# Seven block products for the gate and up projections of three SwiGLUs

## The chip, the cores and the metric

The kernel runs on one NeuronCore of a Trainium2 chip. The metric is the device time of one execution in microseconds (us), less being better. The engines are named as in the profile: PE (TensorE, with its weight loads as PEld), DVE (VectorE), ACT (ScalarE), POOL (GpSimd) and SP (SyncE, which here only issues DMAs).

## The reference

One inference step of two layers over 640 tokens of 1024 features, in float32. Each layer is a SwiGLU, a mixer (layer 0: convolution beside a gated MLP; layer 1: windowed attention) and a second SwiGLU, each with its own norms, shift, scale and gate:

```python
def swiglu(h, wg, wu, wd):
    return (jax.nn.silu(h @ wg) * (h @ wu)) @ wd

def pre(x, m, g, slot):
    h = rms_norm(x, g)
    return h * (1 + m[:, 3 * slot + 1][:, None, :]) + m[:, 3 * slot][:, None, :]

def residual(x, y, m, g, slot, weight):
    return x + weight * m[:, 3 * slot + 2][:, None, :] * rms_norm(y, g)
```

`wg` and `wu` are 1024 x 2816, `wd` is 2816 x 1024. `m` is the modulation, `silu(cond) @ w_mod + b_mod`, for each layer and two condition vectors. There are four SwiGLUs; the code calls them `ffn(l, i)`, in the order (0,0), (0,1), (1,0), (1,1), with the mixers after (0,0) and (1,0).

## The kernel before, in words

Every matmul operand is split into two parts, `hi` and `lo`, so that three matmuls on TensorE (`mm3`: hi*hi, hi*lo, lo*hi) make one product of float32 quality. `h`, the input of a sub-layer, lies with features on partitions: eight chunks `k` of 128 features, each [128, 640 tokens] in two parts. The hidden 2816 features are 22 chunks `j`, in four parts of 5, 5, 6 and 6 (`PARTS`).

For each `j` of an `ffn`, a *unit* is run on the token group GA (tokens 0 to 383) and one on GB (384 to 639). `proj2` does gate and up together: 8 chunks x 2 x 3 = 48 matmuls of 384 columns for GA, 48 of 256 for GB. `glu` empties them: ACT silu of the gate, DVE times the up, ACT copy to `hi`, DVE subtract to `lo`. The weights of `j` come by `wload`: one DMA of 512 KB from SP into a `raw` tile (three of these), ACT makes `hi` (a tile `w`, six slots), DVE makes `lo`. After each unit `background(1)` runs one `mod_chunk`: a 512 KB load of modulation weights into a `raw` tile and two custom DVE reductions of 1024 elements, work for a later sub-layer taken from a queue.

After the chunks of a part the down projection follows: for both halves of the features and the five token tiles, 3 matmuls of 512 columns for each chunk, added to `y` in SBUF by DVE (by ACT copy in the first part). After the last part comes `tail` (or `last_tail` at the very end): `drain` runs what is left in the queue of modulation chunks, then `last(t)` makes the last part's products of token tile t, both halves, adds them to `y`, and the norm of y, the gate row (`ggrow`, a row spread to all partitions by DMA), the residual (`resid`), the norm of x (`scale`) and the transposes into the next `h` (`turn`) follow, woven with the products of the tiles behind.

What sets the order: instructions of PE, DVE and ACT are issued in the order in which they are written (a wrapper, `InOrder`, ties each to the one before). DMAs go to SP's or POOL's queue, where a scheduler places them. Tiles of a kind share a few slots; whoever takes a slot waits for the last reader of the tile that had it.

Of the kernel before, what the change touches and what calls it, by code (L numbers as in the profile page):

```python
# [11 lines left out]
ALU = mybir.AluOpType  # L12
# [65 lines left out]
class Core:  # L78
    """the NeuronCore; tensor, vector and scalar engine in written order"""
# [7 lines left out]
class Builder:  # L87
    def __init__(self, tc, a, ctx):
# [22 lines left out]
    # Slots of a tag are handed out in the order in which their tiles are first written here. Upper and  # L111
    # lower parts come from different engines, so that they have tags of their own.
# [25 lines left out]
    def split(self, src, hi, lo):  # L138
# [45 lines left out]
    def fetch(self, key, dram, nblk, blk=P):  # L184
        """wload ahead of its use; take() returns it"""
# [3 lines left out]
    def fetch_ahead(self, key, dram, nblk, blk=P):  # L189
        """fetch() with the split left to the two closures that are returned: upper part, lower part"""  # L190
# [22 lines left out]
    def proj2(self, ws, h, g, inserts=None):  # L213
        """two projections together, feature chunk by feature chunk; inserts: {k: emitted before chunk k}"""
# [9 lines left out]
    def proj_tok(self, ps, h, w, t):  # L224
        """ps [128 tokens of tile t, n] = h^T w"""
# [5 lines left out]
    def rsqrt_ops(self, ssq, scale, engine=None):  # L231
        """1/sqrt(ssq * scale + eps) on a few columns: the result and the instructions. engine: of the iterations"""
# [3 lines left out]
        # v holds -1/2 of the argument, the first guess comes from its bits  # L236
# [48 lines left out]
    def turn(self, tiles, c):  # L285
        """PSUM [128 features of chunk c, tokens] from the normalised x"""
# [5 lines left out]
    def tail(self, last, nxt, fetches):  # L292
        """last(t): (closures for the last products of the sub-layer for token tile t, [closures that add the two
        halves to y]). Norms, residual and the next sub-layer's input h follow. What is left of h is in four
        dictionaries: closures to be called before the feature chunks of the next sub-layer's first three units on
        GA and of its first on GB. fetches: closures that start the loads of the next sub-layer's first weights
        and return the two closures that split them."""
# [6 lines left out]
        def sq(t, what, s=None):  # L304
            # sum of squares of x or y
# [13 lines left out]
        def both(tx, ty):  # L319
            # the columns of x[tx] and y[ty] together  # L320
# [64 lines left out]
        # the last tile: what follows its products goes between those of the next sub-layer's first three units  # L385
# [9 lines left out]
        def step(tiles=None, c=None):  # L395
            # transposes of a chunk; upper and lower parts of the one before
# [72 lines left out]
    def last_tail(self, last):  # L469
        """as tail(), for the last sub-layer"""  # L470
# [34 lines left out]
    def mod_final(self, l, slot, what):  # L505
        """what: 0 shift and scale, 1 gate"""
# [16 lines left out]
    def gate_rows(self, l, slot):  # L523
        """gg as rows along the features, the same on every partition"""
# [3 lines left out]
        row = self.sm(P, "grow")[:16]  # L528
# [3 lines left out]
        nc.sync.dma_start(out=self.ggrow.rearrange("p a b -> p (a b)"), in_=rows.to_broadcast([P, 2 * D]))  # L532
# [16 lines left out]
    def glu(self, pg, pu, out, g):  # L549
        """out (hi, lo) columns g = silu(pg) * pu"""  # L550
# [6 lines left out]
    def ffn(self, l, i, h, lead, nxt, fetches, started=None):  # L557
        nc, a = self.nc, self.a
# [101 lines left out]
    def conv_gmlp(self, h, lead, nxt, fetches):  # L660
# [46 lines left out]
        def shifted(c):  # L707
            # 32 channels x 4 shifts on the partitions, for the convolution on the tensor engine
# [70 lines left out]
        def mix(c, copy=lambda out, x: nc.scalar.activation(out=out, in_=x, func=AF.Copy)):  # L779
            # position mixing; what follows the products is returned as closures  # L780
# [72 lines left out]
        # LayerNorm over the conv channels, then swish  # L853
# [38 lines left out]
        for n, f in enumerate(parts):  # L892
# [3 lines left out]
            if n == 3:  # L896
                # from here on the products overwrite the normalised channels
# [40 lines left out]
        # the sines have the sign that they need with the partner  # L938
# [7 lines left out]
    def attention(self, h, lead, nxt, fetches):  # L946
# [4 lines left out]
        # keys of chunk 8 + n: latent tiles 1 and 2, cached ones, latent tiles 3 and 4, so that those of any window  # L951
        # lie side by side; the prompt's
# [29 lines left out]
        def rope(s, pos, on_act=False):  # L982
            """closures; the sum of each is left until the products of the next"""
# [660 lines left out]
```

## Time and profile before

| | |
|---|---|
| time, three runs | 2369.91, 2371.31 and 2374.71 us; median 2371.31 |
| span of the profiled execution | 2369.2 us |
| PE busy | 2343.9 us, 99% of the span, 14484 matmuls |
| DVE busy | 1354.3 us, 57% |
| ACT busy | 833.5 us, 35% |
| POOL busy | 111.4 us, 5% |
| HBM | 248.97 MB read, 106 GB/s over the span |
| granted TensorE clock | 0.996 |

The profiled execution has a span of 2369.2 us beside runs of 2369.91 to 2374.71 us, so it stands 2 us below their median. Busy time counts an engine's own instructions; a busy PE is a PE with matmuls in its pipe. In the views, a line names the engine, the operation, output tile, input tiles and their shapes; in a timeline the first two columns are start and duration, in a window table a cell is the busy time with the number of instructions in parentheses. Nearly all instructions carry the line of the `InOrder` helper (L68), so they are told apart by tile names and shapes.

### The profile page before, as it was taken

To read this page: it belongs to the slowest core of one execution; us is meant where nothing else is said; L and a number is where in the kernel's file an instruction comes from. 1 tells how busy PE (TensorE), PEld (TensorE's weight loads), DVE (VectorE), ACT (ScalarE), POOL (GpSimd) and SP (SyncE) were. 2 spreads that over 40 slices of the span, in tenths; PEclk is the share of its full clock that TensorE was granted. 3 is DMA by queue.
4 is the path that set the end of the run, shared out by engine and by line. 5 is a ranking of instruction groups with operands and counts; after the bars stand their busy time and mean duration, and the time that the engine had idled before them with its cause. 6 is when DMAs were issued, how large, how long until landed. Compare 5 with 4: busy or idle time off the path is not lost.

```text
span 2369.2 us, 35411 instructions
## 1 busy us (share of the span) xinstructions
PE 2343.9 (99%) x14484; PEld 2147.5 (91%) x14484; DVE 1354.3 (57%) x2419; ACT 833.5 (35%) x1507; POOL 111.4 (5%) x191
## 2 busy tenths in 40 slices
PE   9999999999999999999999999999899999999998
PEld 7999999999789899989899999998866798989897
DVE  5556665668775566523755666656888652333235
ACT  5322222363354221213532212225468553212122
POOL 1000000021100000000100000002220010000000
PEclk9999999999999999999999999999999999999999
DMA  7343444413223444422224444352000222222221
GB/s 290 117 141 134 152 136 163 137 56 101 73 86 98 134 159 131 147 87 90 67 89 139 151 142 160 134 171 75 28 21 17 92 76 85 72 81 81 80 73 70
DMA packets 85026, 256.82 MB, mean 108 GB/s; under 512 B 9824, under 2 KB 11744, under 8 KB 84096
## 3 DMA queue, kind: packets, MB, share of 16 engines
q1 hardware_dynamic: 83984, 252.74, 32.0%
q8 instruction: 113, 1.85, 0.3%
q0 software_dynamic: 880, 1.83, 0.2%
q14 instruction: 49, 0.40, 0.1%
HBM read 248.97 MB, written 2.93 MB: 106 GB/s over the span
## 4 chain that ended last, share of the span: by engine, by line
PE 94%; DVE 3%; POOL 1%; ACT 1%; issue 1%; DMA 1%; SPq 0%; DVEq 0%; POOLq 0%; ACTq 0%
PE ps L68 94%; DVE tmp L68 1%; DVE w L68 1%; DVE Y L68 1%; POOL nwq L68 1%; DVE act L68 0%; DMA X<-x 0%; DVE X L68 0%; DMA act<-wmod 0%; POOL nwy L68 0%; ACT w L68 0%; ACT Y L68 0%; DVE nwy L68 0%; DVE nwq L68 0%; ACT act L68 0%
## 5 line engine op out<-in xcount | busy, mean ns | idle before, releaser
L68 PE MATMUL ps<-act,w 128*128 128x384 f32 (+4 forms) x9984 | 1479.5, 314 | 8.2 <-DVE w L68 6.8
L68 PEld LDWEIGHTS ps<-act,w 128*128 128x128 f32 (+2 forms) x9984 | 1425.0, 186 | 32.8 <-issue 15.8
L68 PE MATMUL ps<-w,act 128*128 128x512 f32 (+1 forms) x3480 | 782.9, 384 | 3.1 <-ACT tmp L68 3.1
L68 PEld LDWEIGHTS ps<-w,act 128*128 128x128 f32 x3480 | 627.4, 189 | 136.3 <-ACT tmp L68 3.5
L68 DVE TENSOR_TENSOR w<-raw,w 128x1024 fp32r<-128x1024 f32 (+1 forms) x313 | 365.1, 1199 | 151.4 <-ACT w L68 149.9
L68 ACT ACTIVATE w<-raw 128x1024 fp32r<-128x1024 f32 (+1 forms) x313 | 315.5, 1030 | 367.5 <-PE ps L68 146.9
L68 DVE CUSTOM_DVE_ANT_0 scr<-raw,cbc 128x1024 bf16<-128x1024 f32 x256 | 312.9, 1222 | 12.0 <-DMA raw<-wmodT 6.9
L68 DVE TENSOR_TENSOR tmp<-tmp,ps 128x384 f32<-128x384 f32 (+1 forms) x176 | 85.7, 487 | 401.2 <-ACT tmp L68 357.1
L68 ACT ACTIVATE tmp<-ps 128x384 f32<-128x384 f32 (+2 forms) x198 | 83.7, 425 | 652.4 <-PE ps L68 652.0
L68 DVE TENSOR_TENSOR act<-tmp,act 128x256 fp32r<-128x256 f32 (+2 forms) x306 | 135.3, 448 | 133.7 <-ACT act L68 132.5
L68 DVE TENSOR_TENSOR Y<-Y,ps 128x512 f32<-128x512 f32 x140 | 95.6, 686 | 192.9 <-PE ps L68 192.7
L68 ACT ACTIVATE act<-tmp 128x256 fp32r<-128x256 f32 (+3 forms) x304 | 128.3, 433 | 124.1 <-DVE tmp L68 123.9
L68 ACT ACTIVATE Y<-ps 128x512 f32<-128x512 f32 (+2 forms) x96 | 50.8, 532 | 147.6 <-PE ps L68 147.1
L68 ACT ACTIVATE tmp<-ps,sh,G 128x256 f32<-128x256 f32 (+1 forms) x120 | 60.3, 525 | 22.7 <-PE ps L68 22.7
L68 ACT ACTIVATE tmp<-Y 128x1024 bf16<-128x1024 f32 (+2 forms) x39 | 35.1, 901 | 71.4 <-DVE Y L68 71.4
L68 DVE SCALAR_TENSOR_TENSOR act<-act,cw,act 128x640 f32<-128x640 f32 (+14 forms) x60 | 54.5, 909 | 1.8
L68 ACT ACTIVATE Y<-X 128x1024 f32<-128x1024 f32 x30 | 31.8, 1059 | 54.3 <-DVE X L68 50.7
L68 PE MATMUL ps<-ident,Y 128*128 128x128 f32 x260 | 46.7, 273 | 2.6 <-DVE Y L68 2.2
L68 DVE CUSTOM_DVE_ANT_0 raw<-ps,ggrow 128x384 f32<-128x384 f32 (+1 forms) x64 | 41.1, 680 | 12.8 <-PE ps L68 11.4
L68 POOL TENSOR_TENSOR nwq<-nwy 128x1 f32<-128x1 f32 (+1 forms) x30 | 17.9, 595 | 613.2 <-DVE nwy L68 611.7
L68 PEld LDWEIGHTS ps<-ident,Y 128*128 128x128 f32 x260 | 34.4, 140 | 11.7 <-DVE Y L68 3.9
L68 ACT ACTIVATE raw<-raw,nmx 128x384 f32<-128x384 f32 (+1 forms) x64 | 42.2, 669 | 1.0 <-DVE nmx L68 0.9
(149 smaller groups left out, 758.6 us busy)
## 6 DMA issues: line engine op xcount, KB each, us to landing
raw<-wmodT SPq DMA_DIRECT2D x128, 512.0 KB, 3.8
raw<-wg SPq DMA_DIRECT2D x88, 512.0 KB, 4.5
raw<-wu SPq DMA_DIRECT2D x88, 512.0 KB, 3.6
raw<-wd SPq DMA_DIRECT2D x80, 512.0 KB, 4.0
act<-wmod SPq DMA_DIRECT2D x24, 256.0 KB, 6.5
ggrow<-grow SPq DMA_DIRECT2D x6, 1024.0 KB, 4.6
raw<-win SPq DMA_DIRECT2D x12, 512.0 KB, 3.7
raw<-wqkv SPq DMA_DIRECT2D x10, 512.0 KB, 3.8
```

Source lines behind the costliest of these rows:

```text
L68: i = method(*args, **kw)
```

## The change

For the last three SwiGLUs, (0,1), (1,0) and (1,1), `ffn` hands over to a new function, `ffn_seven`. The first four chunks (`LEAD`) still run as units. For the chunks j = 4 to 21 the gate and up products of one j, seen as a 2x2 block product (features 0-511 and 512-1023; tokens 0-319 and 320-639), are made by seven block products p1 to p7 in place of eight. Each is 4 feature chunks x 3 matmuls of 320 columns, 84 matmuls for one j.

- **Sums of h.** `block_sums` makes, for each of four pairs of chunks, two new sums of the blocks of `h`, split in two parts: two adds of 640 columns (hi + lo), four operations of 320, two splits of 640. They stand between the feature chunks of the units (1,GB), (2,GB) and (3,GA), one for each feature chunk.
- **Room.** The sums and two more raw tiles (`rawx`) take the SBUF region of `x`, `y` and `ggrow`. `x` is written to DRAM before (5 DMAs of 512 KB), the down projections of the parts go to DRAM (`ys`: ACT copy to a `tmp` tile, then a DMA, adding from the second part on, on POOL's queue), and `hold_xy` brings all back when the last p4 is done: ten loads of y of 256 KB, five of x of 512 KB, then `ggrow` (1 MB).
- **Weights.** A new tensor `ws` in DRAM holds the blocks of gate and up. For each j: `load_gate` (512 KB, raw `g`), `load_sums` (512 KB on SP into `rawx`, then on POOL's queue 512 KB that are added to it in the DMA: raw `s`), and `load_up` (512 KB for two j, raw `u`). DVE makes the sums `t` from s and g (two adds of 512). `g`, `s` and `t` are split for each j, `u` for every second: 3.5 splits for a j in place of 2.
- **Order.** A round of j runs p1(j), p3(j-1), p6(j), p4(j-1), p5(j), p2(j), p7(j); p1, p6, p5 and p3 of a j add up in one PSUM tile, which is copied after p1, p6 and p5 (evacuations e1, e6, e5) and goes through silu after p3 (e3). e2 adds and takes silu, e7 and e4 subtract, then the product and its split. `prep(j+1)` puts the weight work of the next j between these, with `background(1)` once a round.
- Comments and docstrings are gone as well.

```diff
+SEVEN = [(0, 1), (1, 0), (1, 1)]
+LEAD = 4
+HT = T // 2
...
+    def hold_xy(self, saved=None):
+        self.turn_region("xy")
...
+            for t in range(NT):
+                for half in range(2):
+                    hf = slice(half * 512, half * 512 + 512)
+                    self.nc.sync.dma_start(out=self.y[t][:, hf], in_=ys[t, half])
+                self.nc.sync.dma_start(out=self.x[t], in_=xs[t])
...
     def ffn(self, l, i, h, lead, nxt, fetches, started=None):
+        if (l, i) in SEVEN:
+            return self.ffn_seven(l, i, h, lead, nxt, fetches)
...
+        def whole(n, c):
+            t[n] = self.tmp(T)
+            hi, lo = (u.bitcast(F32) for u in h[c])
+            V.tensor_tensor(out=t[n], in0=hi, in1=lo, op=ALU.add)
...
+        return [lambda: whole(0, pair), lambda: whole(1, pair + 4), first, second, lambda: split(2), lambda: split(3)]
...
+        def load_sums(j):
+
+            w = a["ws"][l, i, j]
+            r = self.rawx()
+            nc.sync.dma_start(out=r, in_=w[:, 512:1536])
+            nc.gpsimd.dma_start(out=r.rearrange("p (a b) -> p a b", a=2),
+                                in_=w[:, 1536:2048].unsqueeze(1).to_broadcast([P, 2, 512]), accum_op=ALU.add)
+            raws["s", j] = r
...
+            def s2():
+                t = raws["t", j] = self.raw(D)
+                V.tensor_tensor(out=t[:, 0:512], in0=raws["s", j][:, 512:1024], in1=raws["g", j][:, 512:1024], op=ALU.add)
+
+            def s4():
+                t = raws["t", j]
+                V.tensor_tensor(out=t[:, 512:1024], in0=t[:, 0:512], in1=raws["g", j][:, 0:512], op=ALU.add)
...
+            return [[lambda: load_up(j) if two else None, s2, s4], [g[0]], [g[1], t[0]], [t[1]] + (nxt_g if first else []),
+                    [s[0], lambda: self.background(1)], [s[1], lambda: load_sums(j + 2) if j + 2 < NJ else None],
+                    u + ([] if first else nxt_g)]
...
+        def product(n, j, ps, start, stop):
+            w = wts.pop((n, j))
+            for p in range(4):
+
+                self.mm3(ps, tuple(u[:, p * P:(p + 1) * P] for u in w), moving[n](p), start and p == 0, stop and p == 3,
+                         skip_group_check=True)
...
+        unit(1, GB, sums_between())
+        weights(3)
+        unit(2, GB, sums_between())
+        for g in GROUPS:
+            unit(3, g, sums_between())
+        run(tops)
...
+                if j > j0:
+                    steps = [(p1, j), (p3, j - 1), (p6, j), (p4, j - 1), (p5, j), (p2, j), (p7, j)]
+                else:
+                    steps = [(p1, j), (p2, j), (p6, j), (p7, j), (p5, j), None, None]
...
+                        o = self.tmp(512)
+                        copy(o, ps)
+                        if pi == 0:
+                            nc.sync.dma_start(out=ys[t, half], in_=o)
+                        else:
+                            nc.gpsimd.dma_start(out=ys[t, half], in_=o, accum_op=ALU.add)
...
+                            else:
+                                self.background(2 if t < 3 else 1)
...
+                self.hold_xy((xs, ys))
+                self.spread_rows(rows)
```

The next listings show three places of the engines' orders. Numbers behind names tell tiles of one kind apart.

**ACT, inside ffn(1,1).** Before, one chunk of the part 5 to 9: the `hi` of two weight tiles, then silu and `hi` of the unit on GA, then of the one on GB.

```order
L68 ACTIVATE w_19060<-raw_19058 128x1024
L68 ACTIVATE w_19066<-raw_19064 128x1024
L68 ACTIVATE tmp_19122<-ps_19072 128x384
L68 ACTIVATE act_19070<-tmp_19122 128x384
L68 ACTIVATE tmp_19177<-ps_19127 128x256
L68 ACTIVATE act_19070<-tmp_19177 128x256
```

After, the round of j = 12, the first after a pair of `u` was split. In order: hi of u, e1(12), hi of g for 13, silu e3(11), hi of t for 13 (w_20592), e6(12), hi of the product of 11, hi of s for 13, e5(12), silu e2(12).

```order
L72 ACTIVATE w_20537<-raw_20429 128x1024
L72 ACTIVATE tmp_20572<-ps_20543 128x320
L72 ACTIVATE w_20575<-raw_20541 128x1024
L72 ACTIVATE tmp_20446<-ps_20414 128x320
L72 ACTIVATE w_20592<-raw_20557 128x1024
L72 ACTIVATE tmp_20573<-ps_20543 128x320
L72 ACTIVATE act_20623<-tmp_20446 128x640
L72 ACTIVATE w_20627<-rawx_20409 128x1024
L72 ACTIVATE tmp_20573<-ps_20543 128x320
L72 ACTIVATE tmp_20572<-tmp_20572 128x320
```

Between e1 and e6 of one PSUM tile (ps_20543) stand now two splits of weights and a silu; the slot of w_20592 was that of the u pair before, which p4(11) is the last to read.

**DVE, ffn(0,1) at the start of the third or fourth chunk.** Before: the last steps of the units (1,GB) and (2,GB), `lo` of two weight tiles, then the unit (3,GA).

```order
L68 TENSOR_TENSOR tmp_7272<-tmp_7272,ps_7223 128x256
L68 TENSOR_TENSOR act_6961<-tmp_7272,act_6960 128x256
L68 TENSOR_TENSOR tmp_7327<-tmp_7327,ps_7278 128x256
L68 TENSOR_TENSOR act_7043<-tmp_7327,act_7042 128x256
L68 TENSOR_TENSOR w_7335<-raw_7332,w_7334 128x1024
L68 TENSOR_TENSOR w_7341<-raw_7338,w_7340 128x1024
L68 TENSOR_TENSOR tmp_7396<-tmp_7396,ps_7347 128x384
L68 TENSOR_TENSOR act_7345<-tmp_7396,act_7344 128x384
```

After, the end of the fourth pair of sums, the units (3,GA) and (3,GB), the two adds that make t for j = 4, and `lo` of g (w_7553) and of t (w_7557) for j = 4.

```order
L72 TENSOR_TENSOR tmp_7432<-tmp_7432,tmp_7440 128x320
L72 TENSOR_TENSOR tmp_7432<-tmp_7424,tmp_7432 128x320
L72 TENSOR_TENSOR sum_7458<-tmp_7440,sum_7457 128x640
L72 TENSOR_TENSOR sum_7468<-tmp_7432,sum_7467 128x640
L72 TENSOR_TENSOR tmp_7477<-tmp_7477,ps_7403 128x384
L72 TENSOR_TENSOR act_7401<-tmp_7477,act_7400 128x384
L72 TENSOR_TENSOR tmp_7532<-tmp_7532,ps_7483 128x256
L72 TENSOR_TENSOR act_7401<-tmp_7532,act_7400 128x256
L72 TENSOR_TENSOR raw_7549<-rawx_7229,raw_7227 128x512
L72 TENSOR_TENSOR raw_7549<-raw_7549,raw_7227 128x512
L72 TENSOR_TENSOR w_7553<-raw_7227,w_7552 128x1024
L72 TENSOR_TENSOR w_7557<-raw_7549,w_7556 128x1024
```

The `lo` of g for j = 4, which p1(4) reads, now stands on DVE behind all four pairs of sums and behind both units of chunk 3.

**SP at the end of ffn(1,0).** Before: the last modulation loads, the weights of the last down projection, then the loads of the next sub-layer.

```order
L498 DMA raw_14581<-wmodT 128x1024
L498 DMA raw_14642<-wmodT 128x1024
L159 DMA raw_14651<-wd 128x1024
L159 DMA raw_14657<-wd 128x1024
L159 DMA raw_14663<-wd 128x1024
L159 DMA raw_14669<-wd 128x1024
L159 DMA raw_14787<-wd 128x1024
L159 DMA raw_14793<-wd 128x1024
L159 DMA raw_15072<-wqkv 128x1024
```

After, the end of the loads of y and x, the gate row, and seven loads of modulation chunks, of which five are shown.

```order
L161 DMA Y_15119<-ys_11874 128x512
L162 DMA X_15118<-xs_11172 128x1024
L573 DMA ggrow_15120<-grow_14326 128x2048
L534 DMA raw_15153<-wmodT 128x1024
L534 DMA raw_15159<-wmodT 128x1024
L534 DMA raw_15165<-wmodT 128x1024
L534 DMA raw_15171<-wmodT 128x1024
L534 DMA raw_15177<-wmodT 128x1024
```

Behind the last weights of the down projection now stand two modulation loads, the 15 loads of y and x, the gate row, and seven more modulation loads, where before the next sub-layer's weights followed at once. The queue of modulation chunks holds 48 for ffn(1,0); `ffn_seven` has 39 places for them ahead of `drain` (14 in rounds, 25 in prep and down projections), so nine are left, two of them issued ahead of the loads of y.

More of the change, by code (lines that the diff above doesn't have):

```diff
@@ L99, in __init__ @@
         self.rowp = pool("rowp", 2, space=bass.MemoryType.DRAM)
+        self.region = None
         self.bg = []
@@ L135, in ps, with turn_region, dram, hold_sums @@
         return self.psp.tile([P, 512], F32, tag="ps", name=self.nm("ps"))
+    def turn_region(self, name):
+        if self.region is not None:
+            self.region.release()
+        self.region = self.tc.alloc_tile_pool(name=self.nm(name), bufs=1, reuse_waits="tile")
+    def hold_xy(self, saved=None):
+        self.turn_region("xy")
+        mk = lambda shape, name: self.region.tile(shape, F32, tag=name, name=self.nm(name))
+        X = mk([P, NT, D], "X")
+        self.Y = mk([P, NT * D], "Y")
+        self.ggrow = mk([P, 2, D], "ggrow")
+        self.x = [X[:, t, :] for t in range(NT)]
+        self.y = [self.Y[:, t * D:(t + 1) * D] for t in range(NT)]
+        if saved is not None:
+            xs, ys = saved
+            for t in range(NT):
[3 more added lines that the diff above has]
+                self.nc.sync.dma_start(out=self.x[t], in_=xs[t])
+    def dram(self, shape, name):
+        return self.rowp.tile(shape, F32, tag=self.nm(name), name=self.nm(name), bufs=1)
+    def hold_sums(self):
+        self.turn_region("sums")
+        self.rawx = lambda: self.region.tile([P, D], F32, tag="rawx", name=self.nm("rawx"), bufs=2)
+        side = lambda tag: self.region.tile([P, T], F32R, tag=tag, name=self.nm("sum"), bufs=8)
+        return lambda: (side("sumh"), side("suml"))
     def split(self, src, hi, lo):
@@ L196, in take, with mm3 @@
         return self.fetched.pop(key)
-    def mm3(self, out, w, x, first, last):
+    def mm3(self, out, w, x, first, last, **kw):
         mm = self.nc.tensor.matmul
-        mm(out, w[0], x[0], start=first, stop=False)
-        mm(out, w[0], x[1], start=False, stop=False)
-        mm(out, w[1], x[0], start=False, stop=last)
+        mm(out, w[0], x[0], start=first, stop=False, **kw)
+        mm(out, w[0], x[1], start=False, stop=False, **kw)
+        mm(out, w[1], x[0], start=False, stop=last, **kw)
     def proj(self, w, h, g):
@@ L521, in mod_final, with gate_rows @@
                                    in1=nw(2 * slot + 1), op0=ALU.mult, op1=ALU.mult)
-    def gate_rows(self, l, slot):
+    def gate_rows(self, l, slot, later=False):
         nc = self.nc
@@ L527, in gate_rows @@
         nc.tensor.transpose(ps[:16, :P], self.gg[l][slot].rearrange("p a b -> p (a b)"), self.ident)
-        row = self.sm(P, "grow")[:16]
+        row = self.smallp.tile([P, P], F32, tag="grow", name=self.nm("grow"), bufs=1)[:16]
         nc.scalar.activation(out=row, in_=ps[:16, :P], func=AF.Copy)
@@ L531, in gate_rows, with spread_rows @@
         nc.sync.dma_start(out=rows.rearrange("o (c p) -> (o c) p", p=P), in_=row)
-        nc.sync.dma_start(out=self.ggrow.rearrange("p a b -> p (a b)"), in_=rows.to_broadcast([P, 2 * D]))
+        if not later:
+            self.spread_rows(rows)
+        return rows
+    def spread_rows(self, rows):
+        self.nc.sync.dma_start(out=self.ggrow.rearrange("p a b -> p (a b)"), in_=rows.to_broadcast([P, 2 * D]))
     def queue_mods(self, l, slot, what):
@@ L632, in ffn, with block_sums, first, second @@
                 wd += [self.wload(a["wd"][l, i, jj], 2, 512) for jj in range(j0 + 4, j1)]
+                if nxt is None:
+                    return self.last_tail(self.last_products(gp, wd))
+                return self.tail(self.last_products(gp, wd), nxt, fetches)
+    def block_sums(self, h, pair, sums, out):
+        nc, V = self.nc, self.nc.vector
+        a, b = slice(0, HT), slice(HT, T)
+        t = {}
+        def whole(n, c):
+            t[n] = self.tmp(T)
+            hi, lo = (u.bitcast(F32) for u in h[c])
+            V.tensor_tensor(out=t[n], in0=hi, in1=lo, op=ALU.add)
+        def first():
+            t[2] = self.tmp(T)
+            V.tensor_tensor(out=t[2][:, a], in0=t[0][:, a], in1=t[0][:, b], op=ALU.subtract)
+            V.scalar_tensor_tensor(out=t[2][:, b], in0=t[2][:, a], scalar=-1.0, in1=t[1][:, b],
+                                   op0=ALU.mult, op1=ALU.subtract)
+        def second():
+            t[3] = t[1]
+            V.tensor_tensor(out=t[3][:, a], in0=t[1][:, a], in1=t[2][:, b], op=ALU.add)
+            V.tensor_tensor(out=t[3][:, b], in0=t[0][:, b], in1=t[1][:, b], op=ALU.subtract)
+        def split(n):
+            pr = sums()
+            out[n - 2][pair] = pr
+            self.split(t[n], *pr)
+        return [lambda: whole(0, pair), lambda: whole(1, pair + 4), first, second, lambda: split(2), lambda: split(3)]
@@ L1284, in setup @@
         ld = nc.gpsimd.dma_start
-        X = self.const([P, NT, D], "X")
-        self.Y = self.const([P, NT * D], "Y")
-        self.x = [X[:, t, :] for t in range(NT)]
-        self.y = [self.Y[:, t * D:(t + 1) * D] for t in range(NT)]
+        self.hold_xy()
         ccol = self.const([P, KC, 2], "ccol")
@@ L1308, in setup @@
         self.shift, self.G, self.gg = mk("sh"), mk("G"), mk("gg")
-        self.ggrow = self.const([P, 2, D], "ggrow")
     def setup_cbc(self):
@@ L1536, in program @@
         self.ffn(1, 1, h, lead, None, [])
+        self.region.release()
 def build(tc, a):
@@ L1571, in layout @@
     f["wg"], f["wu"] = kxm(A(ffn_w_gate)), kxm(A(ffn_w_up))
+    up, low = f["wg"][..., 512:], f["wg"][..., :512]
+    f["ws"] = np.concatenate([up, low, f["wu"][..., 512:], f["wu"][..., :512]], -1)
     f["wd"] = C(A(ffn_w_down).reshape(2, 2, NJ, P, D))
```

178 lines of the change are left out of this document (added).

## Prediction

> **What bounds the kernel now.** I read the page first: the busy shares and the chain of work that ended last.
>
> ```profile
> span 2369.2 us, 35411 instructions
> PE 2343.9 (99%) x14484; PEld 2147.5 (91%) x14484; DVE 1354.3 (57%) x2419; ACT 833.5 (35%) x1507; POOL 111.4 (5%) x191
> PE 94%; DVE 3%; POOL 1%; ACT 1%; issue 1%; DMA 1%; SPq 0%; DVEq 0%; POOLq 0%; ACTq 0%
> ```
>
> PE is the bound nearly everywhere, so matmuls taken away are worth their full time, and any wait that PE does not have now costs its full length. The second view is a window table of one chunk's two units (GA, then GB), which gives the price of a matmul:
>
> ```profile
> 1303.21:1311.62 8.41, 8.41 (x50) 8.41 (x49) 5.50 (x8) 2.95 (x5) 0.00 (x0) 1.00 0.52 180
> 1311.62:1317.31 5.69, 5.69 (x50) 5.69 (x50) 3.49 (x6) 0.83 (x3) 0.00 (x0) 1.00 0.33 109
> ```
>
> 48 matmuls of 384 columns in 8.41 us are 175.2 ns each, 48 of 256 in 5.69 us are 118.5 (the counts of 49 and 50 take in neighbours at the edges). A line through both gives 146.9 ns for 320 columns. One chunk j takes 14.10 us with DVE busy 8.99 of it (5.50 + 3.49): DVE has 5 us to spare there, ACT 10. The third view, groups by form, has the prices of what the change adds on these two:
>
> ```profile
> L68 PE MATMUL ps<-act,w 128*128 128x384 f32 x4784 | 868.9, 338 | 0.4 <-DVE act L68 0.2 <-DVE nmx L68 0.2
> L68 DVE TENSOR_TENSOR w<-raw,w 128x1024 fp32r<-128x1024 f32 x297 | 354.6, 1226 | 144.3 <-ACT w L68 142.8 <-PE ps L68 1.0
> L68 DVE CUSTOM_DVE_ANT_0 scr<-raw,cbc 128x1024 bf16<-128x1024 f32 x256 | 312.9, 1222 | 12.0 <-DMA raw<-wmodT 6.9
> L68 ACT ACTIVATE w<-raw 128x1024 fp32r<-128x1024 f32 x297 | 305.9, 1052 | 335.9 <-PE ps L68 143.2 <-DMA raw<-wu 76.1 <-DMA raw<-wd 41.1
> L68 DVE TENSOR_TENSOR act<-tmp,act 128x256 fp32r<-128x256 f32 x172 | 72.6, 425 | 79.3 <-ACT act L68 78.9
> L68 DVE TENSOR_TENSOR act<-tmp,act 128x384 fp32r<-128x384 f32 x92 | 51.4, 559 | 52.8 <-ACT act L68 52.0 <-issue 0.7
> L68 ACT ACTIVATE tmp<-ps 128x384 f32<-128x384 f32 x92 | 44.9, 488 | 299.8 <-PE ps L68 299.6
> L68 ACT ACTIVATE tmp<-ps 128x256 f32<-128x256 f32 x92 | 35.3, 384 | 347.0 <-PE ps L68 347.0
> L68 DVE TENSOR_TENSOR Y<-Y,ggrow 128x512 f32<-128x512 f32 x20 | 13.7, 684 | 0.0
> L68 DVE TENSOR_TENSOR act<-Y,act 128x640 fp32r<-128x640 f32 x8 | 6.6, 825 | 5.5 <-ACT act L68 5.1
> ```
>
> Between the 256 and 384 forms a DVE operation of 320 columns is 0.49 us and an ACT one 0.44. The first row says that a matmul lasts 338 ns where the next begins after 175: its result is out some 0.17 us after its successor could start.
>
> **What is taken away.** Three SwiGLUs x 18 chunks = 54 chunks go from 96 matmuls (14.10 us) to 84 of 320 columns, 84 x 0.1469 = 12.34 us. 54 x 1.76 = **-95.0 us**, all of it on PE. The DVE adds into y in the down projections become ACT copies and DMAs; PE makes such a tile in 15 to 18 matmuls of 512 columns, over 3.4 us, and a copy takes under 0.7, so I cost that at nothing: PE's own products cover it. The DMA behind it holds one of four tmp slots, and is part of a rival below.
>
> **What is added in a round.** DVE in one round: lo of g, s, t 3 x 1.23, half of u 0.61, s2 and s4 2 x 0.68, e2, e7, e4 3 x 0.49, product and split 2 x 0.83: 8.8 us of 12.34. ACT: 3.5 x 1.05 + five of 0.44 + hi 0.75 = 6.6. Neither is the bound by its sum. In 23 rounds (9 in ffn(0,1), 14 in ffn(1,0); the queue is empty in ffn(1,1)) a modulation chunk of 2 x 1.22 and its two read-outs, 2.5 us, brings DVE to 11.3. It then waits in written order for six products too. Nothing in the trace shows such a round; between 0 (it fits) and 2.5 (all of it late) I take 0.33, near the low end since the sum still fits: **+7.6**.
>
> A wait does come from the order. In the rounds after a u pair was split (j = 7, 12, 14, 18, 20), ACT has hi of t(j+1) ahead of e6(j), and that hi needs the slot which p4(j-1) reads last. p5(j), next on PE, adds into the tile that e6 copies. So PE stands from the end of p4 until the result is out, ACT has done hi, done the copy and handed over: 0.17 + 1.05 + 0.44 + 0.1. The last is two hand-overs, from the timeline after a unit that ended at 1303.21:
>
> ```profile
> 1303.06 0.38 ACT L68 ACTIVATE tmp<-ps 128x256 f32<-128x256 f32 x1 [4.15 <-PE ps L68]
> 1303.48 0.42 DVE L68 TENSOR_TENSOR tmp<-tmp,ps 128x256 f32<-128x256 f32 x1 [1.57 <-ACT tmp L68]
> 1303.94 0.42 ACT L68 ACTIVATE act<-tmp 128x256 fp32r<-128x256 f32 x1 [0.49 <-DVE tmp L68]
> 1304.39 0.42 DVE L68 TENSOR_TENSOR act<-tmp,act 128x256 fp32r<-128x256 f32 x1 [0.48 <-ACT act L68]
> ```
>
> Each step starts 0.03 to 0.05 us behind the one it waits for. 15 rounds x 1.76 = **+26.4**; the low end is 15 x 0.6 (if only e6 itself were in the way), the high end 15 x 2.3.
>
> **The sums of h.** DVE works them off in written order from the start of unit (1,GB), with PE busy for 5.69 x 3 + 8.41 = 25.5 us from there. DVE has: the unit before, 1.6 (that timeline, to 1304.81); four pairs at 2 x 0.83 + 4 x 0.49 + 2 x 0.83 = 5.3, 21.1; four units' steps, 5.8 with ACT between; two weight tiles of chunk 3, 2.45; s2, s4, 1.4; lo of g, 1.23: 33.5, which p1(4) needs. With some 0.4 for hand-overs, 8.4 us of PE waiting in each of three SwiGLUs: **+25.2**. The low end is 4.2 each, since s2, s4 and lo of g stand behind the last unit in any case; the high end 11.
>
> **The first chunk of seven products, j = 4.** In (0,1) and (1,0) a modulation chunk stands between the lo of t and of s; its load waits for the raw tile of g and then takes 3.8 us, so p7 and then p3 wait: 3.9 us each, from 0 to 5; **+7.8**, and 0.7 in (1,1).
>
> **The tails.** hold_xy moves 10 x 256 KB, 5 x 512 KB and 1 MB, 6.29 MB, after p4(21). What the DMA engines do when full, and how long single loads take:
>
> ```profile
> 13.00:30.00 17.00, 14.74 (x138) 10.92 (x139) 13.40 (x41) 11.70 (x19) 0.00 (x0) 1.00 1.05 396
> raw<-wmodT SPq DMA_DIRECT2D x128, 512.0 KB, 3.8
> ggrow<-grow SPq DMA_DIRECT2D x6, 1024.0 KB, 4.6
> ```
>
> At 396 GB/s they are 15.9 us, and with the first landing the gate row, last in the queue, is there 18.5 us after the last products begin. Before, in ffn(1,0), these rows (timelines of PE and DVE) show the room:
>
> ```profile
> 1591.18 25.09 PE L68 MATMUL ps<-w,act 128*128 128x512 f32 x108
> 1616.11 0.38 PE L68 MATMUL ps<-ident,Y 128*128 128x128 f32 x2
> 1599.05 1.39 DVE L68 TENSOR_TENSOR Y<-Y,ps 128x512 f32<-128x512 f32 x2 [3.32 <-PE ps L68]
> 1603.43 1.28 DVE L68 SCALAR_TENSOR_TENSOR Y<-Y,nwy,ggrow 128x1024 f32<-128x1024 f32 x1
> 1607.33 1.38 DVE L68 TENSOR_TENSOR Y<-Y,ps 128x512 f32<-128x512 f32 x2 [1.35 <-PE ps L68]
> ```
>
> The residual of tile 0 comes 12.25 us after the start. In ffn(0,1) it comes 6.2 later; 1.35 goes where DVE waited for PE at 1607.33, and PE's later transposes have little slack: **+5** (0 to 6). In ffn(1,0) nine modulation chunks are left for drain, ahead of tile 0's add on DVE, and the loads of seven stand behind the gate row on SP. The first lands some 20 us after the start; seven at 2.5 us of DVE end at 38, the add-to-residual takes 4.4, so the residual comes at 42.4 in place of 12.25. Less 1.35 and a little slack, PE waits **+28** (20 to 33). In ffn(1,1) last_tail needs the gate row 9.9 us earlier than it is there; its first add of a tile comes every 8.3 us with 2.1 idle, so four tiles win 8.4 back: **+2**.
>
> ```profile
> 2327.12 0.69 DVE L68 TENSOR_TENSOR Y<-Y,ps 128x512 f32<-128x512 f32 x1 [3.25 <-PE ps L68]
> 2335.42 0.69 DVE L68 TENSOR_TENSOR Y<-Y,ps 128x512 f32<-128x512 f32 x1 [2.10 <-PE ps L68]
> ```
>
> **The clock after a long wait.** One gap of PE is that long before, 6.57 us up to 1715.47:
>
> ```profile
> 1708.90:1715.50 6.60, 0.03 (x2) 0.03 (x1) 6.45 (x8) 1.83 (x3) 3.19 (x2) 0.68 0.00 1
> 1715.50:1722.00 6.50, 6.25 (x28) 5.60 (x29) 3.45 (x11) 1.65 (x8) 0.00 (x0) 0.53 0.00 0
> 1722.00:1732.00 10.00, 9.87 (x75) 8.54 (x75) 7.19 (x21) 3.73 (x16) 1.71 (x1) 1.00 0.05 16
> ```
>
> The granted clock (third column from the right) is 0.53 for 6.5 us after PE resumes: 3 us lost. I count this for the tail of (1,0) and for the sums of (1,1), **+6**; in the sums of the other two it lies inside what j = 4 waits for anyway. [...]
>
> **The sum.** -95.0 + 7.6 + 26.4 + 25.2 + 8.5 + 35 + 6 = +13.7 us on a span of 2369.2. The profiled execution stands 2 us under the median run, so in terms of runs 2371.3 + 13.7 = **2385 us**.
>
> **Rivals.**
>
> *Faster: the waits in the u rounds are covered.* Place: e6(j) on ACT in 15 rounds. For it speaks that ACT is busy 6.6 of 12.34 us; against it, that the order fixes hi ahead of e6 and that p5 cannot begin without e6. At nothing, 2385 - 26 = 2359. Below 0.53 us for each wait, the kernel is faster than before by over 0.2%.
>
> *Much slower: the adding DMAs.* 42 loads of s in the preps of rounds are added on POOL's queue, 512 KB each, and 60 tiles of 256 KB into ys. From the issue of s(j+2) to s2 there are some 14 us, of which the plain load takes about 4.5 with its issue; so above 9.5 us for an adding DMA, DVE and with it PE wait. The nearest rows are plain loads on that queue:
>
> ```profile
> ggrow<-mask POOLq DMA_DIRECT2D x1, 384.0 KB, 5.0
> ggrow<-rsin POOLq DMA_DIRECT2D x1, 256.0 KB, 2.9
> ```
>
> [...] At 12 us each, 42 x 2.5 = 105 makes 2490; at 10.5, 2427. No row shows an adding DMA, so this is open.
>
> *About the same: the sums cost half.* If DVE's chain is shorter than I add up, down to 4.2 us a SwiGLU, 12.6 goes and the time is 2372.
>
> **How the numbers follow.** 0.2% of 2371, some 4.7 us, is what a measurement of this kernel can tell from no change. The case as summed, 0.54, own range 2366 to 2405 from the ends of the u rounds, the sums and the tail of (1,0); covered u rounds or several waits at their low ends, 0.18, 2340 to 2366; slow adding DMAs, 0.16, 2405 to 2490; the sums at half, 0.12, 2366 to 2377. Faster is the second case: 0.18. Within 0.2% is most of the last one: 0.10. Slower: 0.72. The range 2348 to 2430 leaves out a little of the second case and half of the third.
>
> **What would show it.** Right: a round without u at 12.3 us of PE, one with u at 14.1 and ACT's hi of t ending it; a gap of 8 us on PE ahead of p1(4); a gap of over 25 us in the tail of ffn(1,0), with drain's loads on DVE's waits; no half clock elsewhere. Wrong: waits for adding DMAs (raw s) on DVE, 320-column matmuls slower than 147 ns, or PE resuming at the end of (1,0) within 10 us.

## The result and the profile after

The changed kernel takes 2445.51 us (median of four runs, 2444.18 to 2452.49) against 2371.11: a ratio of 1.0316, 95% interval 1.0301 to 1.0332. It is slower, as forecast, but by 74 us in place of 14, and lies above the range. The profiled execution is the slowest of the four; it has a span of 2450.7 us, 81.5 above that of before. The page's span, busy shares and chain of work that ended last:

```profile
span 2450.7 us, 35312 instructions
PE 2293.0 (94%) x13836; PEld 2077.2 (85%) x13836; DVE 1597.0 (65%) x2701; ACT 1011.4 (41%) x1783; POOL 228.7 (9%) x305
PE 68%; DVE 13%; DMA 9%; ACT 5%; issue 4%; POOL 1%; SPq 0%; DVEq 0%; ACTq 0%; POOLq 0%
```

PE is still busy 94% of a longer span, but only 68% of the chain goes through it. What PE waited for, first in the kernel before (its two largest entries), then after (columns: engine, tile, releaser, us in total, times, longest):

```profile
PE ps L68 <- DVE w L68: 6.8, 2, 6.6
PE ps L68 <- ACT tmp L68: 3.1, 2, 1.6
```

```profile
PE ps L72 <- ACT tmp L72: 63.0, 26, 7.8
PE ps L72 <- DVE Y L72: 32.9, 4, 25.9
PE ps L72 <- DVE w L72: 19.7, 11, 6.5
PE ps L72 <- ACT w L72: 14.0, 3, 4.7
PE ps L72 <- DVE tmp L72: 12.2, 7, 3.1
```

The next two tables cut both executions at the same places, PE alone (window, its length, PE busy, granted clock, DMA share, GB/s). Before: ffn(0,1) from the last products of unit (0,GB) to the first down projection; from there on each down projection with the chunks behind it (5 to 9, 10 to 15, 16 to 21, up to the last products); the tail of ffn(1,0); the first down projection of ffn(1,1) with its chunks 5 to 9.

```profile
729.42:773.33 43.91, 43.91 (x328) 1.00 0.33 103
773.33:878.27 104.94, 104.94 (x633) 1.00 0.44 146
878.27:997.27 119.00, 119.00 (x728) 1.00 0.46 148
997.27:1123.74 126.47, 126.47 (x760) 1.00 0.26 88
1591.18:1664.90 73.72, 72.81 (x379) 1.00 0.24 80
1969.56:2074.54 104.98, 104.98 (x632) 1.00 0.23 76
```

After, the same stretches:

```profile
729.65:784.88 55.23, 45.39 (x315) 0.94 0.33 85
784.88:892.69 107.81, 98.70 (x572) 0.97 0.68 196
892.69:1019.70 127.01, 113.74 (x656) 0.95 0.69 186
1019.70:1141.97 122.27, 116.54 (x688) 1.00 0.59 153
1644.39:1747.61 103.22, 76.38 (x377) 0.86 0.44 159
2060.81:2158.88 98.07, 96.75 (x573) 1.00 0.56 157
```

The last row is what the change was to be everywhere: five chunks in ffn(1,1), with the down projection ahead of them, go from 104.98 to 98.07 us. The same five in ffn(0,1) go the other way, 104.94 to 107.81, and the next six from 119.00 to 127.01; only the last six, where the queue of modulation chunks is empty, gain (126.47 to 122.27). One difference between the two SwiGLUs is the modulation chunks; the first experiment tests whether it is the one that counts.

Where a part begins in ffn(0,1), j = 5 (timelines of SP, DVE, ACT and PE, in this order):

```profile
816.21 0.33 SPq L534 DMA_DIRECT2D raw<-wmodT  x1
824.04 0.33 SPq L534 DMA_DIRECT2D raw<-wmodT  x1
821.51 1.23 DVE L72 CUSTOM_DVE_ANT_0 scr<-raw,cbc 128x1024 bf16<-128x1024 f32 x1 [5.33 <-DMA raw<-wmodT]
827.55 1.22 DVE L72 CUSTOM_DVE_ANT_0 scr<-raw,cbc 128x1024 bf16<-128x1024 f32 x1 [1.98 <-DMA raw<-wmodT]
832.43 0.48 DVE L72 TENSOR_TENSOR tmp<-tmp,ps 128x320 f32<-128x320 f32 x1
832.95 0.47 ACT L72 ACTIVATE tmp<-tmp 128x320 f32<-128x320 f32 x1 [9.96 <-DVE tmp L72]
834.27 0.42 ACT L72 ACTIVATE tmp<-ps 128x320 f32<-128x320 f32 x1
825.63 1.74 PE L72 MATMUL ps<-sum,w 128*128 128x320 f32 x10 [0.32 <-DVE w L72]
834.74 1.70 PE L72 MATMUL ps<-sum,w 128*128 128x320 f32 x5 [7.37 <-ACT tmp L72]
```

Read from the bottom: PE waits 7.37 us for e6(5) on ACT (834.27), which stands behind hi of g and silu e2(5) (832.95), which waits for DVE's e2 (832.43), which stands in written order behind two modulation chunks and what comes between and after them. Their loads were issued at 816.21 and 824.04. With u of this chunk and g of the next one in the three raw tiles, one tile is left: the second load leaves SP only when the reductions of the first are done (824.02). PE works at half clock around these waits (granted clock 0.50); the two stretches here are the one at j = 5, which begins inside the wait, and the one at j = 10, which begins 0.8 us behind a wait of 2.88 us and takes in the next wait, of 7.17 us:

```profile
831.17:838.00 6.83, 3.26 (x12) 0.50 0.80 166
936.99:950.64 13.65, 6.48 (x25) 0.50 0.68 198
```

### The profile page after: what moved, and what is told of

It reads as the page before. It is cut to its first block, busy times and chain, and to the rows that moved or that the text cites. A ratio compares the mean times of both kernels' runs of the same rounds, so it can differ in the third digit from the quotient of the medians.

```text
span 2450.7 us, 35312 instructions
## 1 busy us (share of the span) xinstructions
PE 2293.0 (94%) x13836; PEld 2077.2 (85%) x13836; DVE 1597.0 (65%) x2701; ACT 1011.4 (41%) x1783; POOL 228.7 (9%) x305
## 4 chain that ended last, share of the span: by engine, by line
PE 68%; DVE 13%; DMA 9%; ACT 5%; issue 4%; POOL 1%; SPq 0%; DVEq 0%; ACTq 0%; POOLq 0%
PE ps L72 68%; DMA raw<-wmodT 5%; DVE tmp L72 3%; DVE w L72 3%; ACT w L72 3%; DVE scr L72 2%; ACT tmp L72 1%; DVE Y L72 1%; DMA ggrow<-grow 1%; DMA rawx<-ws 1%; DVE raw L72 1%; POOL nwq L72 1%; DMA Y<-ys 1%; DVE X L72 0%; DVE act L72 0%
## 5 line engine op out<-in xcount | busy, mean ns | idle before, releaser
L72 PE MATMUL ps<-act,w 128*128 128x384 f32 (+5 forms) x6744 | 1031.9, 319 | 30.9 <-ACT w L72 14.0
L72 PEld LDWEIGHTS ps<-act,w 128*128 128x128 f32 (+2 forms) x6744 | 963.0, 186 | 60.7 <-issue 18.1
L72 PE MATMUL ps<-sum,w 128*128 128x320 f32 x2592 | 417.9, 316 | 75.3 <-ACT tmp L72 54.2
L72 PEld LDWEIGHTS ps<-sum,w 128*128 128x128 f32 x2592 | 393.6, 192 | 87.7 <-ACT tmp L72 64.5
L72 ACT ACTIVATE tmp<-ps 128x320 f32<-128x320 f32 (+4 forms) x396 | 182.1, 461 | 446.5 <-PE ps L72 406.8
L72 DVE TENSOR_TENSOR act<-tmp,act 128x256 fp32r<-128x256 f32 (+4 forms) x252 | 126.7, 510 | 121.7 <-ACT act L72 120.6
L72 ACT ACTIVATE act<-tmp 128x256 fp32r<-128x256 f32 (+4 forms) x250 | 117.4, 483 | 210.5 <-DVE tmp L72 210.4
L752 POOL DMA_DIRECT2D rawx<-ws x54 | 65.3, 1218 | 785.9 <-DMA rawx<-ws 374.7
L72 DVE TENSOR_TENSOR tmp<-tmp,ps 128x384 f32<-128x384 f32 (+2 forms) x122 | 58.9, 483 | 82.1 <-ACT tmp L72 78.9
L72 DVE TENSOR_TENSOR w<-rawx,w 128x1024 fp32r<-128x1024 f32 x54 | 66.0, 1222 | 41.7 <-ACT w L72 41.5
L72 PE MATMUL ps<-ident,Y 128*128 128x128 f32 x260 | 47.8, 278 | 33.2 <-DVE Y L72 32.9
```

The costliest lines, as they stand in the source:

```text
L72: i = method(*args, **kw)
L752: nc.gpsimd.dma_start(out=r.rearrange("p (a b) -> p a b", a=2), in_=w[:, 1536:2048].unsqueeze(1).to_broadcast([P, 2, 512]), accum_op=ALU.add)
```

## The experiments

**The loads alone.** The 80 modulation loads of the three SwiGLUs are left out. The reductions keep their place and time, but read a row that is in SBUF already.

```diff
-        raw = self.raw(D)
-        nc.sync.dma_start(out=raw, in_=self.a["wmodT"][l, ch])
+        if l == 1 or ch >= 64:
+            raw = self.cbc[:, 0, :]
+        else:
+            raw = self.raw(D)
+            nc.sync.dma_start(out=raw, in_=self.a["wmodT"][l, ch])
```

> The modulation reductions of the three changed SwiGLUs read a row that is in SBUF already, so their 80 loads of 512 KB and their raw tiles are left out, their DVE time stays. Theory (the loads): at the first chunk of a part, e2(j0) stands on DVE behind reductions whose loads wait for one of three raw tiles; p5(j0) waits for it by way of ACT. Then the gaps of 7.5 us on PE ahead of p5(5), p5(10) and the 3.7 us ahead of p5(16) are gone with the half clock behind them (55 us), j = 4 of two SwiGLUs gains some 4 us each, and the tail of ffn(1,0) 14 us, since nine chunks of 2.5 us are left but no loads: 2368 us (2358 to 2380). Rival (DVE's time): the reductions themselves are too much there, the gaps stay at 4 us or more: above 2400 us. Second rival (the adding DMAs): nothing changes at the parts' starts, 2430 us.

2383.95 us, ratio 1.0058 (1.0036 to 1.0081). DVE's wait for modulation loads and PE's for ACT's copies, after and then here:

```profile
DVE scr L72 <- DMA raw<-wmodT: 91.2, 31, 11.5
```

```profile
DVE scr L72 <- DMA raw<-wmodT: 2.1, 2, 1.9
PE ps L72 <- ACT tmp L72: 32.8, 28, 2.0
PE ps L72 <- DVE Y L72: 19.8, 4, 15.1
```

DVE is as busy as in the changed kernel (1594.8 us, there 1597.0). Yet the first rounds of the five parts that begin with modulation chunks, which took 51.5 us more than their products, now take no more than these, and the longest wait for ACT is 2.0 us. So it is the loads and their tiles, not DVE's time. The result lies 4 us above the end of the range expected: the tail of ffn(1,0) still waits 15.1 us, with nine chunks of 2.5 us ahead of the first add.

**The adding loads.** The 54 adding DMAs of s are left out (the block sums of the weights lack that part).

```diff
-            nc.gpsimd.dma_start(out=r.rearrange("p (a b) -> p a b", a=2),
-                                in_=w[:, 1536:2048].unsqueeze(1).to_broadcast([P, 2, 512]), accum_op=ALU.add)
```

> The changed kernel without the 54 adding loads into s on POOL's queue; the sums of the weights lack that part. Theory (modulation loads and raw tiles make the waits, the adding loads take 7.9 us in the trace and have 14): 2440 us (2434 to 2447). Rival (the adding loads hold up s2 or slow the other loads): 2425 us or less.

2441.87 us, ratio 1.0294 (1.0275 to 1.0312): some 4 us, and the interval overlaps that of the changed kernel. Four of the five waits at the parts' starts are as long as before, 7.4 to 7.9 us; the fifth falls from 3.5 to 2.0. So the second rival of the prediction is not the cause of the loss here. The adding DMAs into ys were left in; PE has no wait inside a down projection.

**The clock.** Matmuls whose result nobody reads keep PE busy in the waits at five parts' starts.

```diff
+        used = [None]
...
+            used[0] = w
...
+                        if j == j0 and f[0] is p5 and j0 > LEAD and self.bg:
+                            spare = self.ps()[:, :HT]
+                            for _ in range(46 if j0 < 16 else 24):
+                                nc.tensor.matmul(spare, used[0][0][:, 0:P], h[0][0][:, 0:HT], start=True, stop=True)
```

> The changed kernel with 46 (in the last part 24) matmuls of 320 columns that nobody reads put on PE ahead of p5(j0) in the five parts' starts that wait; they fill some 6.7 of the 7.5 us. Theory (the half clock behind a wait costs what the trace shows as work done at half clock there, 12 to 13 us): 2433 us (2428 to 2438). Rival (PE waits for DVE afterwards in any case, so its clock does not matter): 2445 us.

2437.46 us, ratio 1.0273 (1.0254 to 1.0292). Mean granted clock, after and here:

```profile
core 0: 2450.7 us, clock 0.971
```

```profile
core 0: 2438.8 us, clock 0.982
```

Useless work makes the kernel 8 us faster by the medians, 10 by the ratios. In the trace of the changed kernel PE does 25 us of work at half clock at these five starts, which by estimate costs 12.6 us (at j = 5 it had 12 matmuls in 3.26 us there, 0.27 us each, against 84 in the 12.00 us behind, 0.14); here no half clock is left there. Why the gain is somewhat smaller, no run shows.

**Modulation chunks away from the parts' starts.** They go into the first half of the down projection.

```diff
-                    [s[0], lambda: self.background(1)], [s[1], lambda: load_sums(j + 2) if j + 2 < NJ else None],
+                    [s[0]] + ([] if first else [lambda: self.background(1)]), [s[1], lambda: load_sums(j + 2) if j + 2 < NJ else None],
...
-                                self.background(2 if t < 3 else 1)
+                                self.background(2)
...
-                            if t == 4:
-                                self.background(1)
```

> The one modulation chunk in the prep of a part's first chunk and the one at the end of a down projection are moved ahead, into the first half of the down projection (eight there in place of six); the one in prep(4) goes to the end of the queue. Theory (loads in the way of e2): gaps ahead of p5(j0) gone, j = 4 of two SwiGLUs faster by 4 us each, 2.5 us more in the tail of ffn(1,0): 2393 us (2385 to 2410). Rival (too little room for DVE in a down projection): g and t of j0 come late instead, p1(j0) or p6(j0) waits 3 us or more: above 2425 us.

2421.27 us, ratio 1.0217 (1.0188 to 1.0247), between the two theories: a gain of 24 and not 52. The first rounds of the five parts are down from 51.5 us above their products to 9.6, but some 19 us come back in the rounds behind them and 3 in the tail of ffn(1,0). Two of the new waits, of 3.7 and 4.2 us, stand ahead of p5(6). There it is the sum s(7) that comes late (timelines of SP, POOL and DVE of this kernel):

```profile
820.36 0.33 SPq L751 DMA_DIRECT2D rawx<-ws  x1
826.35 1.19 POOL L752 DMA_DIRECT2D rawx<-ws  x1 [48.83 <-DVE w L72]
835.20 0.69 DVE L72 TENSOR_TENSOR raw<-rawx,raw 128x512 f32<-128x512 f32 x1 [4.00 <-issue]
```

From the plain load at 820.36 to DVE's s2 at 835.20 pass 14.8 us, 8.9 of them from the issue of the adding load. That is the limit of 14 us that the prediction gave to its second rival; it is reached once the first wait is out of the way. The profile names no releaser for these 4 us, but it has the landing of this adding load: 8.8 us behind its issue at 826.35, less than 0.1 us ahead of s2. So the adding load ends this wait. What all such waits cost is not shown, since the adding loads were left out of the changed kernel alone and not of this one.

**The tail of ffn(1,0).** The 16 chunks of (1,1,0) join the queue of ffn(0,1), whose drain leaves what is not done of them (`keep` is 16 there and 0 later).

```diff
-        for l, s, w in ((0, 2, 1), (1, 0, 0), (1, 0, 1)):
+        for l, s, w in ((0, 2, 1), (1, 0, 0), (1, 0, 1), (1, 1, 0)):
...
+        self.keep = 16
...
-        while self.bg:
+        while len(self.bg) > self.keep:
```

> The first modulation slot of layer 1 is queued with ffn(0,1), which has seven places free, and what is left of it goes on to ffn(1,0): two chunks are left for drain there in place of nine. Theory (drain's loads behind the gate row): the gap of 26 us in the tail of ffn(1,0) shrinks to some 5 us, while the part of chunks 16 to 21 of ffn(0,1) gets gaps as the others: 2431 us (2425 to 2438). Rival (the reload of x, y and the gate row itself): the gap stays above 20 us, 2450 us.

2430.04 us, ratio 1.0254 (1.0225 to 1.0284), as the theory had it. PE's waits for DVE's y fall from 32.9 us to:

```profile
PE ps L72 <- DVE Y L72: 10.0, 4, 4.3
```

and the part of chunks 16 to 21 of ffn(0,1) takes 7 us more, since it now meets modulation chunks at its start.

**The u rounds.** Only t's hi is moved behind e6.

```diff
-                    [g[0]], [g[1], t[0]], [t[1]] + (nxt_g if first else []),
+                    [g[0]], [g[1]], [t[0], t[1]] + (nxt_g if first else []),
```

> Only the hi of t(j+1) is moved on ACT behind e6(j). Theory: the 15 to 16 gaps of 1.5 us ahead of p5 after a u pair go, 2422 us (2417 to 2430). Rival: t comes late for p6(j+1) and the wait only moves: 2440 to 2450 us.

2441.70 us, ratio 1.0304 (1.0274 to 1.0333): some 4 us by the medians, and the interval overlaps that of the changed kernel. In ffn(1,1) the rounds behind j = 4 run without a wait up to p4(21). In the SwiGLUs with modulation chunks p6 now waits 0.5 to 1.6 us in most rounds. It waits for e1 on ACT, which stands behind silu e2; that waits for DVE's e2 (3.10 us in the round of j = 7), and e2 stands behind the reductions of a modulation chunk. So the wait moves, as the rival has it, but not by way of a late t. Each theory holds in one kind of SwiGLU.

**ffn(1,1) alone.**

```diff
-SEVEN = [(0, 1), (1, 0), (1, 1)]
+SEVEN = [(1, 1)]
```

> Seven products in ffn(1,1) alone; the other two SwiGLUs as before the change. ffn(1,1) has no modulation chunks. Theory (the seven products pay by themselves, the loss is in what they meet): the differences by stage of the changed kernel for this SwiGLU, +7.3, -6.9, -4.7 and +1.9 us, add up to -2.4: 2367.5 us (2365 to 2370). Rival (the form itself loses): 2375 us or more.

2370.36 us, ratio 0.9990 (0.9981 to 0.9999), 0.4 us above the range expected: the gain is small or nothing, and the waits are those of the changed kernel in this SwiGLU (4.7 us ahead of p1(4), 1.3 in the u rounds, 3.1 ahead of p4(21)).

**ffn(1,1) alone, three moves.** t behind e6; the split for j = 4 ahead of unit (3,GB); the fourth weight tile of the down projection behind e7.

```diff
-        for g in GROUPS:
-            unit(3, g, sums_between())
+        unit(3, GA, sums_between())
         run(tops)
+        left = prep(LEAD)
+        run([f for fs in left[:-1] for f in fs])
+        left = left[-1]
+        unit(3, GB)
...
-                    ahead = [[] for _ in range(3)] + [wd[n:n + 1] for n in range(4)]
+                    ahead = [[] for _ in range(3)] + [wd[n:n + 1] for n in range(3)] + [[]]
...
-            run(wd[4:5])
+            run(wd[3:5])
```

> As only_last, with three moves: hi of t(j+1) behind e6(j) on ACT; the weights of j = 4 split ahead of the unit (3,GB) in place of behind it; the fourth weight tile of a down projection split behind e7. Theory: the five to seven waits of 1.5 us (9), the wait ahead of p1(4) with its half clock (7), the 3.24 us ahead of p4(21) and two of 0.5 (5) go: 2347 us (2343 to 2354). Rival (each wait is followed by the next one in line): 2360 us or more.

2352.71 us, ratio 0.9917 (0.9903 to 0.9930), the fastest kernel of this study, 20 us under the one before, as that ran beside it:

```profile
PE 2317.0 (99%) x14268; PEld 2119.3 (90%) x14268; DVE 1433.6 (61%) x2513; ACT 894.9 (38%) x1599; POOL 150.9 (6%) x229
PE ps L72 <- ACT w L72: 3.3, 1, 3.3
```

PE is at 99% again. The waits in the u rounds and ahead of p4(21) are gone (0.4 us is left of the latter); of the 4.7 us ahead of p1(4), 3.3 remain, as before for ACT's hi of g.

**One move more.** Against the kernel with three moves, g of j = 4 is split ahead of unit (3,GA).

```diff
+        left = prep(LEAD)
+        run([f for fs in left[:3] for f in fs])
         unit(3, GA, sums_between())
         run(tops)
-        left = prep(LEAD)
-        run([f for fs in left[:-1] for f in fs])
+        run([f for fs in left[3:-1] for f in fs])
...
```

> only_last_tuned with the two adds that make t and the split of g for j = 4 moved once more, ahead of the unit (3,GA) and of the last sums. Theory (p1(4) waits for nothing but the split of g): the 3.4 us ahead of p1(4) and the half clock behind it (2.4 us) go, 2347 us (2344 to 2350). Rival (the sums then come late and p6(4) waits as long): 2351 to 2354 us.

2356.81 us, ratio 0.9932 (0.9918 to 0.9946): no gain, and by the medians 4 us slower than with three moves, though the intervals overlap. As the rival has it, p1(4) waits no longer, but p6(4) does, for e1 and not for the sums; the time lies 3 us above the rival's range (timeline of PE):

```profile
1967.70 2.77 PE L72 MATMUL ps<-sum,w 128*128 128x320 f32 x9 [5.99 <-ACT tmp L72]
```

ACT's e1, which p6 needs, now stands behind the splits of t and s, the steps of unit (3,GB), one of which waits for DVE, and the hi of u. The wait has changed its place.

**All together in three SwiGLUs.** The three moves of only_last_tuned (t behind e6 only where no modulation chunks are queued), start_mods_moved and seven_mods_earlier together. The diff shows only the line that moves t, which all kernels with the three moves have.

```diff
+            early = len(self.bg) > 0
...
+                    [g[0]], [g[1]] + t[:early], t[early:] + (nxt_g if first else []),
```

> All three SwiGLUs with these moves (t behind e6 only where no modulation chunks are queued), the modulation chunks ahead of a part's start moved as in start_mods_moved, and seven of them moved to ffn(0,1) as in seven_mods_earlier. Theory (the costs add up): 2445 - 24 - 15 - 20 - 12 - 11 = 2363 us (2350 to 2380). Rival (DVE and the raw tiles are full in the rounds with modulation chunks, so what is taken from one place comes back in the next): above 2390 us.

2395.43 us, ratio 1.0098 (1.0074 to 1.0122), above the theory's range and in the rival's. DVE still waits for modulation loads, and PE for ACT and DVE:

```profile
DVE scr L72 <- DMA raw<-wmodT: 57.9, 30, 14.2
PE ps L72 <- ACT tmp L72: 41.5, 29, 3.9
PE ps L72 <- DVE Y L72: 24.2, 4, 18.9
```

The waits ahead of p5 move from the part's first round to its second (2.8 to 3.9 us). In four of these five rounds DVE's s2 begins 0.1 us behind the landing of an adding load, as in start_mods_moved. With fewer places for modulation chunks four are left for the tail of ffn(1,0), which waits 18.9 us. The gains do not add up: behind each wait that goes stands another, on the raw tiles, on DVE's written order or on an adding load. How much of the 32 us above the theory each of them holds is not shown.

## Why the prediction was wrong, and where it was right

The ledger of the profiled executions, by the steps of the prediction (measured: time of a product's stretch above 12.34 us for a chunk, read from the start of each product, half clock included):

| step | predicted, us | measured, us |
|---|---|---|
| 54 chunks | -95.0 | -95 (a clean round 12.28 to 12.30) |
| u rounds and modulation rounds | +26.4, +7.6 | +26 in 15 u rounds, +2 more |
| waiting ahead of p1(4) | +25.2 | +14.4 |
| j = 4, with its half clock | +8.5, and 3 of the clock | +20.6 |
| starts of parts 5, 10, 16 | 0 | +51.5, and 3.7 in the rounds behind |
| ends of parts | 0 | +14.3 |
| tails | +35, and 3 of the clock | +40.5 (6.6, 29.5, 4.4) |
| down projections, attention, remainder | 0 | +3 |

**What was right.** The pace of 320 columns (146.9 ns predicted; 84 matmuls in 12.29 us are 146.3), and that the waits eat the gain. The u rounds are as the order said: hi of t, then e6's copy, then PE (timelines of ACT and PE in the round of j = 7).

```profile
857.80 1.06 ACT L72 ACTIVATE w<-raw 128x1024 fp32r<-128x1024 f32 x1 [2.48 <-PE ps L72]
858.76 0.42 ACT L72 ACTIVATE tmp<-ps 128x320 f32<-128x320 f32 x1
859.24 2.03 PE L72 MATMUL ps<-sum,w 128*128 128x320 f32 x12 [1.32 <-ACT tmp L72]
```

The tail of ffn(1,0) is as walked through, with seven modulation loads behind the gate row on SP, and PE 26 us behind (rows of SP, DVE and PE):

```profile
1655.99 0.32 SPq L573 DMA_DIRECT2D ggrow<-grow  x1
1657.34 19.53 SPq L534 DMA_DIRECT2D raw<-wmodT  x7
1666.41 1.23 DVE L72 CUSTOM_DVE_ANT_0 scr<-raw,cbc 128x1024 bf16<-128x1024 f32 x1 [11.54 <-DMA raw<-wmodT]
1696.59 0.69 PE L72 MATMUL ps<-ident,Y 128*128 128x128 f32 x2 [25.95 <-DVE Y L72]
```

**The step that failed.** The modulation chunks of the parts' starts were priced at nothing. The prediction priced the chunk in prep(4) at 3.9 us and the 23 in rounds at 0.33, and said nothing of those that prep(5), prep(10) and prep(16) and the ends of the down projections put in the same place. They cost 51.5 us in the first rounds of five parts and 3.7 in the rounds behind, most of the 68 us by which the profiled execution lies above the sum. mods_resident shows that it is their loads and the tiles for these: without them the five first rounds take no more than their products. The mechanism had been named for j = 4 (a load that waits for a raw tile, with DVE's written order behind it) and the same walk leads to it in the other parts. Of the down projection the prediction walked only the copies and their DMAs, and these PE's products do cover; what they did not cover are the modulation loads that DVE waits for as the next part begins.

**Terms mis-sized.** j = 4 at 20.6 in place of 8.5, some 8 of it the half clock. The clock as a whole: the sum had 6 us for two places; in the trace half clock costs 36 us (half of the 71.9 us that PE was busy at a granted clock of 0.50), 32 more than in the kernel before (half of 8.7). All nine waits of PE over 4.5 us (4.6 to 26.0) had it inside or behind them, and so had some as short as 1.6, while others of up to 3.1 us had none. The ends of parts: e7(21) on DVE stands behind lo of a weight tile whose hi waits on ACT, 3.1 us of waiting ahead of each p4(21), not looked for at all (rows of DVE and PE):

```profile
1138.42 1.22 DVE L72 TENSOR_TENSOR w<-raw,w 128x1024 fp32r<-128x1024 f32 x1 [1.48 <-ACT w L72]
1139.57 0.48 DVE L72 TENSOR_TENSOR tmp<-ps,tmp 128x320 f32<-128x320 f32 x1
1140.10 2.03 PE L72 MATMUL ps<-sum,w 128*128 128x320 f32 x12 [3.08 <-DVE tmp L72]
```

The sums of h were priced too high, 8.4 for 4.8 us each (1.1 more, until lo of g is there, stands under j = 4): DVE's four pairs take 5.0 each and not 5.3, and the steps of the units overlap with them more than I added up; it came out near the low end. The modulation rounds, too, cost less than their 7.6. These two terms are some 16 us too high between them and hide as much of what is missing.

The measured time lies in the span that the prediction gave to slow adding DMAs, but by another cause: leaving these loads out of the changed kernel gained some 4 us. One of its signs of being wrong did appear, waits of DVE for the adding loads: there are four, 12.7 us together and the longest 4.5.

**On the clock.** The prediction took 3 us for a place from its row of the kernel before. Here the clock was at half for 6.83 us with PE busy 3.26 of it, 1.6 us lost, at the start of part 5; and for 13.65 us with PE busy 6.48 of it, 3.2 us lost, at part 10, where a wait of 2.88 us had come just before. In the two places that the sum counted, 2.5 us were lost in the tail of ffn(1,0) (half clock for 27.31 us, PE busy 4.98 of it) and 2.1 in j = 4 of ffn(1,1) (6.83 us, PE busy 4.29), both less than the 3 us of the row.

## What to carry to other kernels

When matmuls are taken from a kernel whose PE is at 99%, the engines beside it must do more in less time, and a wait in their written order can become PE's (here PE's waits for ACT's tmp went from 3.1 to 63.0 us): walk through every place where a piece of the new order begins or ends, not one of each kind, and follow background work there with its load, its tile and what stands behind it. A saving is best tried first where nothing else shares the buffers: here the SwiGLU without background work gained 20 us after three moves of order, and with the two others changed as well every arrangement tried stayed slower than the kernel before. In the trace of the changed kernel each of the nine waits of PE over 4.5 us cost twice, as a wait and as work at half clock.

## What the runs showed of the hardware

An adding DMA of 512 KB on POOL's queue took 7.9 us from issue to landing (median of 54), against 4.1 for the plain load into the same tiles from SP's queue, and one of 256 KB into DRAM took 4.7. Stretches at half clock lasted 6.83 and 13.65 us at the starts of parts 5 and 10, and from 3.41 to 27.31 us in the whole trace of the changed kernel. In another run 46 matmuls whose result nobody read, put into each of four waits, with 24 in a fifth, raised the mean granted clock from 0.971 to 0.982 and made the kernel 8 us faster.
